# Half-row second passes in the scores of an encoder block: two query tiles side by side, odd tiles with the low part first

## The chip, the cores and the metric

The kernel runs on one core of a Trainium2 chip. The metric is the device time of one execution in microseconds (us), as the median of several runs. TensorE multiplies matrices, VectorE and ScalarE do elementwise work and read the accumulators in PSUM, GpSimd does elementwise work in SBUF, and SyncE issues most transfers.

## The reference

One encoder block over 1024 tokens of 1024 features, in float32: a layer norm, one wide projection, two attention branches, gates, an output projection, a second layer norm, a squared-ReLU MLP and a third layer norm. What matters here are the scores of the two branches:

```python
proj = h @ w_in[l] + b_in[l]
qa, ka, va, qb, kb, vb, ga, gb = jnp.split(proj, IN_SPLITS, axis=-1)
...
s = jnp.einsum('bwhd,bkwjhd->bhwkj', qr, kn).astype(jnp.float32) * scale
s = s + bias.astype(jnp.float32)[None]
...
s = jnp.einsum('bnqgrd,bnkgd->bngrqk', qb, kb).astype(jnp.float32) * (Dh ** -0.5)
s = jnp.where(valid[None, :, None, None], s, MASK_VALUE)
```

The first is neighbourhood attention (NA, 8 heads) on a 16 x 64 grid with a learned bias, the second windowed attention (SWA, 8 query heads, 2 key heads, rotary positions, a sink logit). Heads have 64 features.

## The kernel before, in words

Matmuls run in float32r, which keeps fewer bits than float32. Each operand is therefore split in a high part (the value rounded to float32r) and a low part (what the rounding left off), and a product is made of several matmuls that add up in PSUM. Weights and activations of the projections take three (`gemm3_steps`, L261: high x high, high x low, low x high, for 8 slices of the features).

Since a head has 64 features and TensorE takes 128 rows, the scores stack the parts. The tile `q` (128 x 1024) holds the high part of the queries in rows 0 to 63 and the low part in rows 64 to 127, or the other way round for the odd heads of SWA. The tiles `kh` and `kl` hold the keys' high and low part, each written twice, in both halves of the rows. A first pass `q` x `kh` (L506) then sums high x high and low x high, and a second pass `q` x `kl` (L507) adds high x low and low x low.

*Order of the work.* The attention stage lies about between 95 and 465 us. There are 64 steps: 16 heads (first 8 of SWA, then 8 of NA) times 4 pairs `t` of query tiles of 128 tokens. A tile looks at three tiles of keys (384 columns), the first and the last tile at two (256); so a step with t of 0 or 3 has one tile of each width, and the others have two of 384. `steps` (L717) works as a software pipeline whose order on every engine is as written:

- `part_a2(s + 1)` (L532): VectorE normalises the probabilities of the next step (L540, L543).
- `part_a(s + 2)` (L495): TensorE makes the scores of both tiles, each in a bank `ps_s` of its own (there are two), and VectorE adds bias or mask and takes the maximum (L509), which frees the bank; then the negated, scaled maximum goes to `st` (L513, L515).
- `pump` (L665): TensorE does some matmuls of the projections that later heads need, 12 a step in the SWA heads and 18 in the NA heads. They fill its time between the attention's matmuls.
- `part_b(s)` (L545): TensorE transposes the probabilities (L564), ScalarE copies them out (L567), VectorE makes the low part (L570). In between, `part_e(s + 2)` has ScalarE do the exponentials (L527, and L530 for the sinks).
- `part_c(s - 1)` (L573): probabilities x values (L599); at every second pair ScalarE (L605) and VectorE (L606) evacuate the output.

*How the queries come about.* A projection of 512 tokens (a half of the sequence) fills one bank `ps_mm`; there are two such banks, so the bank is asked for again one projection later. For NA (`proj_na_qk`, L312), 64 rows of the bank are queries and 64 are keys. ScalarE writes the queries' high part (L324) and the keys' high part twice (L325, L326); a few pumps later VectorE writes the queries' low part (L329) and the keys' low part (L331, which is the bank's last reader, and L333, a copy). For SWA (`proj_swa_q`, L403), one projection gives two heads; ScalarE evacuates the bank at once (L369), VectorE and GpSimd apply the rotary positions in SBUF, and some pumps later ScalarE copies the high parts (L414, two instructions, one a head) and VectorE subtracts for the low parts (L419, two instructions). All these are deferred by counts of pumps (`defer`, L274; D_NA, D_ROPE) and sit in the engines' queues between the steps' own instructions. Weights of the next projection are split on ScalarE (L457) and VectorE (L462).

Of the kernel before, what the change touches and what calls it, by code (L numbers as in the profile page):

```python
# [12 lines left out]
AF = mybir.ActivationFunctionType  # L13
ALU = mybir.AluOpType

P = 128
# [23 lines left out]
C_R = 98  # L40
N_PAR = 146

# [33 lines left out]
def encoder_block(ctx, tc, x, w_in, w_na, w_swa, w_out, w_ff1, w_ff2, par, rows, rpbp, sink,  # L76
# [4 lines left out]
    def b32(ap):  # L81
        return ap.bitcast(F32)
# [225 lines left out]
    def cols_na(h):  # L308
        return [(0, 8, 0, 64, w_in[:, h * 64:(h + 1) * 64]),
                (0, 8, 64, 64, w_in[:, 512 + h * 64:512 + (h + 1) * 64])]  # L310

    def proj_na_qk(h, w, store):  # L312
        q = ap.tile([P, S], F32R, tag="q", name="q", bufs=3)
        kh = ap.tile([P, S], F32R, tag="kh", name="kh")
        kl = ap.tile([P, S], F32R, tag="kl", name="kl")
        store.append((q, kh, kl))
        bq, bk = prm[0:64, C_QK + h:C_QK + h + 1], prm[64:P, C_QK + h:C_QK + h + 1]
        for half in range(2):
            cs = slice(half * 512, (half + 1) * 512)
            ps = psum("mm")  # L320
            yield from gemm3_steps(ps, w, lambda part, k: h_perm(part, k, half))

            def evac(cs=cs, ps=ps):
                ACT.activation(q[0:64, cs], ps[0:64, :], AF.Identity, bias=bq, scale=1.0)  # L324
                ACT.activation(kh[64:P, cs], ps[64:P, :], AF.Identity, bias=bk, scale=1.0)  # L325
                ACT.activation(kh[0:64, cs], ps[64:P, :], AF.Identity, bias=bk, scale=1.0)  # L326

            def evac2(cs=cs, ps=ps):
                DVE.scalar_tensor_tensor(out=q[64:P, cs], in0=ps[0:64, :], scalar=bq, in1=b32(q[0:64, cs]),  # L329
                                         op0=ALU.add, op1=ALU.subtract)  # L330
                DVE.scalar_tensor_tensor(out=kl[64:P, cs], in0=ps[64:P, :], scalar=bk, in1=b32(kh[64:P, cs]),  # L331
                                         op0=ALU.add, op1=ALU.subtract)
                DVE.tensor_copy(kl[0:64, cs], b32(kl[64:P, cs]))  # L333
            defer(0, evac, D_NA, evac2)
# [68 lines left out]
    def proj_swa_q(hp, w, store):  # L403
        qs = [ap.tile([P, S], F32R, tag="q", name="q", bufs=3) for _ in range(2)]
        store.extend(qs)
        for half in range(2):
            cs = slice(half * 512, (half + 1) * 512)
            ps = psum("mm")
            yield from gemm3_steps(ps, w, lambda part, k: h_nat(part, k, half))

            def hi(qf, cs=cs):
                for i in range(2):
                    a = slice(i * 64, i * 64 + 64)
                    ACT.copy(qs[i][a, cs], qf[a])  # L414

            def lo(qf, cs=cs):
                for i in range(2):
                    a, b = slice(i * 64, i * 64 + 64), slice(64 - i * 64, 128 - i * 64)
                    DVE.tensor_tensor(out=qs[i][b, cs], in0=qf[a], in1=b32(qs[i][a, cs]), op=ALU.subtract)  # L419
            rope(ps, prm[:, C_QB + hp:C_QB + hp + 1], half, (hi, lo))  # L420
# [74 lines left out]
    def part_a(s):  # L495
# [3 lines left out]
        st = ap.tile([P, 8], F32, tag="st", name="st", bufs=4)  # L499
        pns = []  # L500
        for i in range(2):
            j = 2 * t + i
            c0, c1 = max(j - 1, 0), min(j + 2, 8)
            n = (c1 - c0) * P
            ps = psum("s")
            PE.matmul(ps[:, :n], q[:, j * P:(j + 1) * P], kh[:, c0 * P:c1 * P], start=True, stop=False)  # L506
            PE.matmul(ps[:, :n], q[:, j * P:(j + 1) * P], kl[:, c0 * P:c1 * P], start=False, stop=True)  # L507
            p = ap.tile([P, 384], F32, tag="ss", name="ss", bufs=6)
# [1458 lines left out]
```

## Time and profile before

| What | us |
|---|---|
| Median of 3 runs | 1359.37 (1358.86 to 1360.43) |
| The profiled execution | 1356.82 |
| Its span in the trace | 1355.0 |
| TensorE busy | 1328.8 |
| VectorE busy | 991.9 |
| ScalarE busy | 705.1 |
| GpSimd busy | 275.4 |

The granted clock of TensorE is 0.998 over the span. The span is what lies between the first and the last instruction in the trace. PE is TensorE, DVE VectorE, ACT ScalarE, POOL GpSimd. A row of a group gives line, engine, operation, output<-inputs, shapes and count, then busy us and the mean ns of one, then the idle time before it and what ended that. Matmuls are pipelined and their ends are modelled, so that a busy TensorE isn't TensorE at its peak; the distance from one start to the next says more.

### The profile page before, as it was taken

Reading aid. Unit: us, or ns where it says so; the run is one execution under the profiler, and the core shown is the slowest. Engines: PE = TensorE matmul, PEld = TensorE weight load, DVE = VectorE, ACT = ScalarE, POOL = GpSimd, SP = SyncE. Lnnn points to the kernel's source line nnn. Section 1 sums busy time; section 2 is a strip of 40 time slices with the busy share of each in tenths; the row PEclk is TensorE's granted clock in tenths of the full one; section 3 lists DMA queues with packets and bytes.
Section 4 is the critical chain, followed back from the end, with each engine's and each line's share of the span. In section 5 each row is a group of like instructions: output and inputs, shape, how many; then the busy total and the mean of one; then the engine's idle time right before and its main releaser. Section 6 shows DMA issues by size and latency. Waiting matters only on the chain.

```text
span 1355.0 us, 17359 instructions
## 1 busy us (share of the span) xinstructions
PE 1328.8 (98%) x6299; PEld 1096.0 (81%) x6299; DVE 991.9 (73%) x1624; ACT 705.1 (52%) x1223; POOL 275.4 (20%) x260
## 2 busy tenths in 40 slices
PE   8999999999999999999999999999999999999997
PEld 6788888888888878888888788888887788888885
DVE  7658989877877896443678977677655668787777
ACT  5446667665665535531446755555554533333346
POOL 3322212121120000333630012222100001111207
PEclk9999999999999999999999999999999999999999
DMA  6531021112111433665244565665529554544323
GB/s 222 170 121 34 24 63 44 25 35 52 40 28 39 125 98 118 212 192 203 87 140 132 182 226 198 210 201 184 198 93 328 191 187 148 209 148 169 127 101 125
DMA packets 135798, 183.94 MB, mean 136 GB/s; under 512 B 27168, under 2 KB 85920, under 8 KB 132000
## 3 DMA queue, kind: packets, MB, share of 16 engines
q1 hardware_dynamic: 134992, 182.17, 40.6%
q8 instruction: 49, 0.80, 0.2%
q10 hardware_dynamic: 720, 0.67, 0.1%
q14 instruction: 37, 0.30, 0.1%
HBM read 126.69 MB, written 56.31 MB: 135 GB/s over the span
## 4 chain that ended last, share of the span: by engine, by line
PE 74%; DVE 16%; ACT 5%; issue 2%; DMA 2%; POOL 1%; SPq 0%; DVEq 0%; ACTq 0%; POOLq 0%
PE ps_mm L267 13%; PE ps_mm L1715 6%; PE ps_o L1283 6%; PE ps_mm L1283 6%; PE ps_t L1283 5%; PE ps_s L1715 5%; PE ps_t L1715 4%; PE ps_o L1715 4%; PE ps_s L1283 2%; DVE ss L543 2%; DVE ss L509 2%; ACT ss L527 2%; PE ps_o L599 2%; PE ps_mm L820 1%; PE ps_t L564 1%
## 5 line engine op out<-in xcount | busy, mean ns | idle before, releaser
L267 PE MATMUL ps_mm<-hT,whi 128*128 128x512 f32 x832 | 274.3, 404 | 6.2 <-POOL hT L243 3.3
L267 PEld LDWEIGHTS ps_mm<-hT,whi 128*128 128x128 f32 x832 | 154.0, 190 | 37.0 <-POOL hT L243 4.7
L267 PE MATMUL ps_mm<-hT,wlo 128*128 128x512 f32 x416 | 169.9, 408 | 1.0 <-DVE wlo L658 1.0
L527 ACT ACTIVATE ss<-ss,st 128x384 f32<-128x384 f32 (+1 forms) x128 | 74.5, 585 | 65.5 <-DVE st L515 34.7
L1583 ACT CAST t<-stg 128x2048 fp32r<-128x2048 f32 x28 | 53.4, 1908 | 87.6 <-PE ps_o L1715 47.0
L1715 PE MATMUL ps_mm<-t,t 128*128 128x512 f32 x384 | 91.7, 394 | 2.3 <-DVE t L1586 2.0
L1734 POOL TENSOR_TENSOR acc<-acc,rst 128x512 f32<-128x512 f32 x16 | 31.3, 1953 | 299.2 <-DMA rst<-xr_d 286.3
L1715 PE MATMUL ps_s<-t,t 128*128 128x512 f32 x384 | 90.8, 392 | 0.0
L267 PEld LDWEIGHTS ps_mm<-hT,wlo 128*128 128x128 f32 x416 | 78.8, 189 | 12.7 <-DVE wlo L658 1.4
L1715 PEld LDWEIGHTS ps_mm<-t,t 128*128 128x128 f32 x384 | 71.9, 188 | 19.6 <-DVE t L1586 2.9
L567 ACT CAST pth<-ps_t 128x384 fp32r<-128x384 f32 (+1 forms) x128 | 51.9, 456 | 66.1 <-PE ps_t L564 65.6
L1715 PEld LDWEIGHTS ps_s<-t,t 128*128 128x128 f32 x384 | 72.1, 188 | 16.1
L1283 PE MATMUL ps_t<-hS,tw 128*128 128x512 f32 x348 | 84.3, 391 | 0.0
L1283 PEld LDWEIGHTS ps_t<-hS,tw 128*128 128x128 f32 x348 | 65.3, 188 | 14.3
L1586 DVE TENSOR_TENSOR t<-stg,t 128x2048 fp32r<-128x2048 f32 x28 | 65.4, 2334 | 14.8 <-ACT t L1583 14.8
L1105 POOL TENSOR_TENSOR mx<-sg 128x512 f32<-128x512 f32 x16 | 33.5, 2094 | 190.6 <-DVE sg L1104 190.6
L1715 PE MATMUL ps_t<-t,t 128*128 128x512 f32 x288 | 68.8, 393 | 0.1
L1715 PE MATMUL ps_o<-t,t 128*128 128x512 f32 x288 | 67.8, 391 | 0.0
L570 DVE TENSOR_TENSOR ptl<-ps_t,pth 128x384 fp32r<-128x384 f32 (+1 forms) x128 | 61.1, 517 | 7.4 <-ACT pth L567 7.1
L1715 PEld LDWEIGHTS ps_t<-t,t 128*128 128x128 f32 x288 | 53.8, 188 | 13.1 <-DVE t L1586 1.3
L1715 PEld LDWEIGHTS ps_o<-t,t 128*128 128x128 f32 x288 | 54.1, 188 | 11.8
L1474 DVE TENSOR_TENSOR usl<-usl 128x512 f32<-128x512 f32 x64 | 50.8, 794 | 14.9 <-ACT usl L1367 11.7
(300 smaller groups left out, 3138.4 us busy)
## 6 DMA issues: line engine op xcount, KB each, us to landing
us_d<-usl SPq DMA_DIRECT2D x112, 256.0 KB
stg<-us_d SPq DMA_DIRECT2D x28, 1024.0 KB
raw<-in_w_ff SPq DMA_DIRECT2D x36, 512.0 KB
raw<-in_w_in SPq DMA_DIRECT2D x20, 512.0 KB
sg<-sg_d SPq DMA_DIRECT2D x32, 256.0 KB
w2b<-in_w_ff SPq DMA_DIRECT2D x7, 1024.0 KB
w2a<-in_w_ff SPq DMA_DIRECT2D x5, 1024.0 KB
sg_d<-sa SPq DMA_DIRECT2D x16, 256.0 KB
```

The costliest lines, as they stand in the source:

```text
L267: PE.matmul(ps, a[:, k, :], act(b, k), start=(k == 0 and i == 0), stop=(k == NK - 1 and i == 2))
L509: DVE.tensor_tensor_reduce(out=p[:, :n], in0=ps[:, :n], in1=bias_of(j), scale=1.0, scalar=NEG, op0=ALU.add, op1=ALU.max, accum_out=st[:, i ...
L527: ACT.activation(p[:, :n], p[:, :n], AF.Exp, bias=st[:, 2 + i:3 + i], scale=0.125, accum_out=st[:, 4 + i:5 + i])
L567: ACT.copy(pth[:, a:b, :], pv)
L570: DVE.tensor_tensor(out=ptl[:, a:b, :], in0=pv, in1=b32(pth[:, a:b, :]), op=ALU.subtract)
L1105: POOL.tensor_tensor(out=mx[:, f, half * 512:(half + 1) * 512], in0=both[0], in1=both[1], op=ALU.add)
L1283: PE.matmul(ps, ww, act[:, part, k, :], start=(first and k == 0 and m == 0), stop=(k == 3 and m == 2), skip_group_check=True)
L1474: DVE.tensor_tensor(out=out, in0=a, in1=b, op=op)
L1583: ACT.copy(slot[:, :, 0, :], src)
L1586: DVE.tensor_tensor(out=slot[:, :, 1, :], in0=src, in1=b32(slot[:, :, 0, :]), op=ALU.subtract)
L1715: PE.matmul(ps, st[:, a, part, j * P:(j + 1) * P], w[:, a, wpart, :], start=(first and a == 0 and m == 0), stop=(a == 3 and m == 2), skip_ ...
L1734: POOL.tensor_tensor(out=z, in0=z, in1=t, op=ALU.add)
```

## The change

Four things are changed.

1. `part_a` first makes the first pass of both tiles and then the second pass of both. The second pass takes only 64 of the 128 rows: rows 0 to 63 for the even tile of the step and rows 64 to 127 for the odd one. It adds high x low; low x low, which the full pass added, is no longer computed. The two second passes use different halves of the array's rows and different banks.
2. For that, the high part of the queries has to lie in rows 0 to 63 in even tiles and in rows 64 to 127 in odd tiles, for every head. `parity` picks the even or the odd tiles of a half of the sequence, as two blocks of 128 tokens.
3. In `proj_na_qk`, ScalarE's one write of the high part (64 x 512) becomes two of 64 x 256, and VectorE's one write of the low part becomes two. The bias of the queries is needed in rows 64 to 127 too, so the parameter table gets 8 columns (C_QO).
4. In `proj_swa_q`, ScalarE still copies the whole high part per head and then copies one parity of it into the other rows (64 x 256, one more instruction a head). VectorE's one subtraction per head becomes two of 64 x 256; one of them writes over the high part that it has read.

```diff
+    def parity(t, half, odd):
+        return t[:, half * 512:(half + 1) * 512].rearrange("p (j o f) -> p j o f", o=2, f=P)[:, :, odd]
...
         bq, bk = prm[0:64, C_QK + h:C_QK + h + 1], prm[64:P, C_QK + h:C_QK + h + 1]
+        bo = prm[64:P, C_QO + h:C_QO + h + 1]
...
-            def evac(cs=cs, ps=ps):
-                ACT.activation(q[0:64, cs], ps[0:64, :], AF.Identity, bias=bq, scale=1.0)
+            def evac(cs=cs, ps=ps, half=half):
+                for odd, rows_ in enumerate((slice(0, 64), slice(64, P))):
+                    ACT.activation(parity(q[rows_], half, odd), parity(ps[0:64], 0, odd), AF.Identity, bias=bq, scale=1.0)
...
-            def evac2(cs=cs, ps=ps):
-                DVE.scalar_tensor_tensor(out=q[64:P, cs], in0=ps[0:64, :], scalar=bq, in1=b32(q[0:64, cs]),
-                                         op0=ALU.add, op1=ALU.subtract)
+            def evac2(cs=cs, ps=ps, half=half):
+                for odd, (hi, lo, b) in enumerate(((slice(0, 64), slice(64, P), bq), (slice(64, P), slice(0, 64), bo))):
+                    DVE.scalar_tensor_tensor(out=parity(q[lo], half, odd), in0=parity(ps[0:64], 0, odd), scalar=b,
+                                             in1=parity(b32(q[hi]), half, odd), op0=ALU.add, op1=ALU.subtract)
...
-            def hi(qf, cs=cs):
-                for i in range(2):
-                    a = slice(i * 64, i * 64 + 64)
-                    ACT.copy(qs[i][a, cs], qf[a])
-
-            def lo(qf, cs=cs):
+            def hi(qf, cs=cs, half=half):
                 for i in range(2):
                     a, b = slice(i * 64, i * 64 + 64), slice(64 - i * 64, 128 - i * 64)
-                    DVE.tensor_tensor(out=qs[i][b, cs], in0=qf[a], in1=b32(qs[i][a, cs]), op=ALU.subtract)
+                    ACT.copy(qs[i][a, cs], qf[a])
+                    ACT.copy(parity(qs[i][b], half, 1 - i), parity(qf[a], 0, 1 - i))
+
+            def lo(qf, half=half):
+                for i in range(2):
+                    a, b = slice(i * 64, i * 64 + 64), slice(64 - i * 64, 128 - i * 64)
+                    for odd, to in ((i, b), (1 - i, a)):
+                        DVE.tensor_tensor(out=parity(qs[i][to], half, odd), in0=parity(qf[a], 0, odd),
+                                          in1=parity(b32(qs[i][a]), half, odd), op=ALU.subtract)
...
-        pns = []
+        pns, pss_ = [], []
...
-            ps = psum("s")
-            PE.matmul(ps[:, :n], q[:, j * P:(j + 1) * P], kh[:, c0 * P:c1 * P], start=True, stop=False)
-            PE.matmul(ps[:, :n], q[:, j * P:(j + 1) * P], kl[:, c0 * P:c1 * P], start=False, stop=True)
+            pss_.append((psum("s"), j, c0, c1, n))
+            PE.matmul(pss_[i][0][:, :n], q[:, j * P:(j + 1) * P], kh[:, c0 * P:c1 * P], start=True, stop=False)
+        for i, (ps, j, c0, c1, n) in enumerate(pss_):
+            rows_ = slice(i * 64, i * 64 + 64)
+            PE.matmul(ps[:, :n], q[rows_, j * P:(j + 1) * P], kl[rows_, c0 * P:c1 * P], start=False, stop=True)
+        for i, (ps, j, c0, c1, n) in enumerate(pss_):
```

The places that the change moves in the engines' queues are these. TensorE in a step with t = 3 of an SWA head, before (`ps_s` are the score banks, `ps_mm` a projection's, `kh` and `kl` the keys' parts, the last number the columns; the shape is the output's):

```order
L267 MATMUL ps_mm<-hT,wlo 128x512
L267 MATMUL ps_mm<-hT,whi 128x512 x2
L506 MATMUL ps_s<-kh,q 128x384
L507 MATMUL ps_s<-kl,q 128x384
L506 MATMUL ps_s<-kh,q 128x256
L507 MATMUL ps_s<-kl,q 128x256
L267 MATMUL ps_mm<-hT,wlo 128x512
L267 MATMUL ps_mm<-hT,whi 128x512 x2
```

and now:

```order
L268 MATMUL ps_mm<-hT,wlo 128x512
L268 MATMUL ps_mm<-hT,whi 128x512 x2
L519 MATMUL ps_s<-kh,q 128x384
L519 MATMUL ps_s<-kh,q 128x256
L522 MATMUL ps_s<-kl,q 128x384
L522 MATMUL ps_s<-kl,q 128x256
L268 MATMUL ps_mm<-hT,wlo 128x512
L268 MATMUL ps_mm<-hT,whi 128x512 x2
```

The second tile's first pass has moved ahead of the first tile's second pass, and the two second passes stand next to each other.

ScalarE between the exponentials of an SWA step and the next, where the second half of a pair of heads' queries is copied, before:

```order
L527 ACTIVATE ss,st<-ss,st 128x256
L530 ACTIVATE st<-st,snk 128x2
L414 CAST q<-qf 64x512 x2
L567 CAST pth<-ps_t 128x384 x2
L527 ACTIVATE ss,st<-ss,st 128x256
L527 ACTIVATE ss,st<-ss,st 128x384
L530 ACTIVATE st<-st,snk 128x2
L605 COPY oT<-ps_o 64x512
```

and now:

```order
L543 ACTIVATE ss,st<-ss,st 128x256
L546 ACTIVATE st<-st,snk 128x2
L424 CAST q<-qf 64x512
L425 CAST q<-qf 64x2x128
L424 CAST q<-qf 64x512
L425 CAST q<-qf 64x2x128
L583 CAST pth<-ps_t 128x384 x2
L543 ACTIVATE ss,st<-ss,st 128x256
L543 ACTIVATE ss,st<-ss,st 128x384
L546 ACTIVATE st<-st,snk 128x2
```

Two copies of 64 x 2 x 128 have come in ahead of the casts (`pth`) that a VectorE subtraction waits for.

VectorE at an evacuation of an NA projection, before (`oT` is the attention's output, `q` and `kl` the queries and the keys' low part):

```order
L570 TENSOR_TENSOR ptl<-ps_t,pth 128x384 x2
L606 TENSOR_TENSOR oT<-ps_o,oT 64x512
L329 SCALAR_TENSOR_TENSOR q<-ps_mm,prm,q 64x512
L331 SCALAR_TENSOR_TENSOR kl<-ps_mm,prm,kh 64x512
L333 CAST kl<-kl 64x512
```

and now:

```order
L586 TENSOR_TENSOR ptl<-ps_t,pth 128x384 x2
L622 TENSOR_TENSOR oT<-ps_o,oT 64x512
L339 SCALAR_TENSOR_TENSOR q<-ps_mm,prm,q 64x2x128 x2
L341 SCALAR_TENSOR_TENSOR kl<-ps_mm,prm,kh 64x512
L343 CAST kl<-kl 64x512
```

The bank's last reader, once L331 and now L341, stands behind two half-wide instructions instead of one whole one.

More of the change, by code (lines that the diff above doesn't have):

```diff
@@ L40 @@
 C_R = 98
-N_PAR = 146
+C_QO = 146
+N_PAR = 154
 N_AHEAD = 4
@@ L1946 @@
                                       a["b_ff2"][0])),
+        np.roll(qk, 64, axis=0),
     ], axis=1)
```

## The prediction

> **What bounds the kernel now.** I read the page first for the whole, then the waits and the chain of waits of the attention stage (95 to 465 us, where all 128 edited matmuls lie), then durations by shape and the timeline at the edited places.
>
> ```profile
> span 1355.0 us, 17359 instructions
> PE 1328.8 (98%) x6299; PEld 1096.0 (81%) x6299; DVE 991.9 (73%) x1624; ACT 705.1 (52%) x1223; POOL 275.4 (20%) x260
> ```
>
> By busy time TensorE is the bound, but its ends are modelled, so that says little. The waits of the stage are more telling (waiter, what it waited for, total us, times, longest):
>
> ```profile
> PE ps_s L506 <- DVE st L509: 2.4, 3, 1.2
> PE ps_mm L267 <- DVE kl L331: 2.1, 5, 1.1
> ```
>
> TensorE hardly waits, and where it does, it is for VectorE to give back a bank of PSUM: the score bank in the first half of the stage, the projection bank in the second. The chain of waits (start, us, engine, tile, line) shows which engine sets the pace in between. First the windowed (SWA) heads:
>
> ```profile
> 108.20 0.34 PE ps_t L564 x3
> ```
>
> ```profile
> 171.76 0.34 DVE ss L509
> ...
> 172.40 1.20 ACT ss L527 x4
> ...
> 263.82 0.77 DVE kl L331
> 264.63 0.73 PE ps_mm L267 x2
> ```
>
> Up to 108.2 us TensorE leads. From there to 264.6 us I take the path as a loop between VectorE and ScalarE: reduction (L509), exponential (L527), scaling (L543), and VectorE's other work in its fixed order; TensorE runs ahead and is stopped once per pair of heads. Only from 131 to 157 us does the chain name TensorE, and I read that as a tie, since the ScalarE copy that is said to wait for it there starts just as ScalarE's instruction before it ends:
>
> ```profile
> 156.68 0.28 ACT L530 ACTIVATE st<-st,snk 128x2 f32<-128x2 f32 x1
> 156.98 0.58 ACT L605 COPY oT<-ps_o 64x512 f32<-64x512 f32 x1
> ```
>
> In the neighbourhood (NA) heads the pattern is another:
>
> ```profile
> 300.57 0.34 PE ps_t L564 x3
> ...
> 300.99 0.86 ACT pth L567 x2
> ...
> 302.94 0.57 ACT q L324
> ...
> 304.94 0.74 DVE q L329
> ...
> 310.19 0.57 ACT q L324
> ...
> 313.50 0.74 DVE q L329
> ...
> 314.26 0.77 DVE kl L331
> ...
> 315.07 0.73 PE ps_mm L267 x2
> ```
>
> TensorE leads from 264.6 to 300.9, then 14 us of ScalarE and VectorE, two evacuations of projections among them (L324, L329), lead until the bank comes back at 315.07. The cycle comes three times, once per pair of heads (with the last two evacuations of the SWA part these are the five waits of the row above); after it TensorE leads.
>
> **The change part by part.** *TensorE.* What a second pass costs is the distance from its start to the next start:
>
> ```profile
> 305.07 0.28 PE L507 MATMUL ps_s<-kl,q 128*128 128x256 f32 x1
> 305.19 0.34 PE L506 MATMUL ps_s<-kh,q 128*128 128x384 f32 x1
> 305.37 0.34 PE L507 MATMUL ps_s<-kl,q 128*128 128x384 f32 x1
> 305.54 0.39 PE L267 MATMUL ps_mm<-hT,wlo 128*128 128x512 f32 x1
> ```
>
> 0.12 us at 256 columns, 0.17 at 384. If the two half-row matmuls of a step run beside each other, the shorter is hidden: 32 steps (t of 1 or 2) save 0.17 and 32 save 0.12, 9.3 us in all, 0.145 a step. No row of before has a 64-row matmul; the bounds are 0.145 saved and, with the array emptied at both switches, a loss: the last row but one is busy 0.34 for 0.17 of distance, so emptying is about 0.17, twice 0.34, less 0.145 is 0.195 lost a step. I take the saving, since the narrow matmuls that the kernel already mixes in show no such gap:
>
> ```profile
> 302.90 0.28 PE L599 MATMUL ps_o<-pth,vv 128*128 128x256 f32 x1
> 303.02 0.28 PE L599 MATMUL ps_o<-ptl,vv 128*64 128x256 f32 x1
> ```
>
> 0.12 apart, like two full ones of 256 columns. (That is 64 columns, not 64 rows, so the row is near, not the same.) The Trainium skill, "TensorE: Matmul & The Clock Gate", Part 3, says that matmuls on different row groups run concurrently, starting about 4 ns apart; no run here shows it, and by it the saving is the one I take.
>
> The new order also lets VectorE's first reduction of a step start up to 0.17 us later (three matmuls ahead of it instead of two) and asks for the second score bank 0.17 earlier. In SWA VectorE comes to its reductions after they are ready, and in NA the loop's next lead is TensorE's own, so both cost nothing; without that cover they would cost 0.17 a step where VectorE waits for scores.
>
> *VectorE and ScalarE.* Every write of the queries' two parts is cut in two of half the width, and the windowed queries get an extra copy. Prices:
>
> ```profile
> L570 DVE TENSOR_TENSOR ptl<-ps_t,pth 128x384 fp32r<-128x384 f32 x96 | 50.2, 550 | 5.9 <-ACT pth L567 5.7
> L570 DVE TENSOR_TENSOR ptl<-ps_t,pth 128x256 fp32r<-128x256 f32 x32 | 13.3, 417 | 1.5 <-ACT pth L567 1.4
> L567 ACT CAST pth<-ps_t 128x384 fp32r<-128x384 f32 x96 | 43.0, 483 | 58.8 <-PE ps_t L564 58.5
> L567 ACT CAST pth<-ps_t 128x256 fp32r<-128x256 f32 x32 | 12.0, 375 | 7.3 <-PE ps_t L564 7.1
> L329 DVE SCALAR_TENSOR_TENSOR q<-ps_mm,prm,q 64x512 fp32r<-64x512 f32 x16 | 11.9, 745 | 3.5 <-ACT kh L326 3.2
> L324 ACT ACTIVATE q<-ps_mm,prm 64x512 fp32r<-64x512 f32 x16 | 10.8, 674 | 0.1
> L414 ACT CAST q<-qf 64x512 fp32r<-64x512 f32 x12 | 7.3, 611 | 0.1
> L419 DVE TENSOR_TENSOR q<-qf,q x16: 684/687/1676, 87.2 to 218.4; 64x512 fp32r<-64x512 f32 x16
> ```
>
> VectorE's slope is (550-417)/128 = 1.04 ns an element, ScalarE's (483-375)/128 = 0.84; 256 elements fewer are 266 and 216 ns. So a half of L419 is 687-266 = 421 and the pair costs +0.155 us; a half of L329 is 479, the pair +0.21; a half of L324 is 458, the pair +0.24; the extra copy is 611-216 = 395, two of them +0.79 a half of SEQ. Bounds for a half-wide instruction: half the old price (nothing added) and a whole one.
>
> *SWA, 108 to 264.6.* VectorE sets the pace, so TensorE's saving there is worth nothing, and the 4 steps before 108 give -0.58. VectorE's additions count in full: six halves of queries fall here, 12 x 0.155 = 1.86; the first four NA evacuations, 4 x 0.21 = 0.85; ScalarE's 0.24 once, where L605 and behind it VectorE's L606 queue behind L324 just before 264.6. The extra copies stand ahead of the casts that VectorE subtracts from:
>
> ```profile
> 133.12 1.23 ACT L414 CAST q<-qf 64x512 fp32r<-64x512 f32 x2
> 134.38 0.86 ACT L567 CAST pth<-ps_t 128x384 fp32r<-128x384 f32 x2
> ...
> ```
>
> ```profile
> 135.31 1.01 DVE L570 TENSOR_TENSOR ptl<-ps_t,pth 128x384 fp32r<-128x384 f32 x2
> ```
>
> Moved by 0.79, the first cast ends at 134.38+0.79+0.48 = 135.65 where VectorE wants it at 135.31: +0.34, three times (one half in each pair of heads; at the other half VectorE comes to the casts later, and I add nothing): 1.0. Sum: 1.86+0.85+0.24+1.0-0.58 = +3.4.
>
> *NA, three cycles.* In the 14 us that ScalarE and VectorE lead, two evacuations add 2 x (0.24+0.21) = +0.90. In the part that TensorE leads, a bank that came back just in time now comes late:
>
> ```profile
> 286.50 0.68 DVE L606 TENSOR_TENSOR oT<-ps_o,oT 64x512 f32<-64x512 f32 x1 [1.75 <-ACT oT L605]
> 295.73 0.42 DVE L570 TENSOR_TENSOR ptl<-ps_t,pth 128x256 fp32r<-128x256 f32 x1 [0.26 <-ACT pth L567]
> ...
> 297.45 0.76 DVE L331 SCALAR_TENSOR_TENSOR kl<-ps_mm,prm,kh 64x512 fp32r<-64x512 f32 x1
> ```
>
> ```profile
> 298.43 0.62 PE L267 MATMUL ps_mm<-hT,whi 128*128 128x512 f32 x2
> ```
>
> L331 ends at 298.21, the bank is used again at 298.43: 0.22 of room. Two evacuations stand in that chain too: VectorE waits for ScalarE behind each (the rows at 286.50 and 295.73), so L331 ends 2 x (0.24+0.21) = 0.90 later, 0.68 past the old use, whatever TensorE saved since the first of the two. The three steps before that save 0.44, and one after the bank's return 0.15. A cycle: -0.44+0.68-0.15+0.90 = +0.99, three +3.0. If that bank stays in time, the cycle is about nothing (six steps, -0.87, against +0.90). The last six steps, TensorE's own, save 0.87.
>
> Sum: 3.4+3.0-0.9 = +5.5 us. The profiled execution took 1356.8 us (span 1355.0 and 1.8 around it), 2.6 under the median of the three runs, 1359.4. Forecast: 1359.4+5.5 = 1364.9. The parameter table's 8 more columns are one transfer long before; I cost them at nothing.
>
> **The rivals.** *Faster.* The halves cost half (no fixed part shows at 64 partitions), ScalarE's copies hide, and only TensorE's saving is left where it leads: -0.58, 3 x -0.87, -0.87 is -4.1, 1355.3. For it: TensorE is 98% busy and named by most of the chain. Against: each pair of widths above shows a fixed part. With the additions (9.6 us between this sum and the forecast's) scaled by f, the total is -4.1+9.6f: it turns at f = 0.43.
>
> *It cancels.* f between 0.15 and 0.7, so that the total is within 2.7 us of 1359.4; or all prices hold and the bank used at 298.43 stays in time in every cycle (3.4+0.1-0.9 = +2.6, 1362.0).
>
> *Serial.* The half-row matmuls queue one behind the other, as the old ones did: nothing saved, SWA +3.95, each cycle 0.68+0.90, three 4.7: +8.7, 1368.1.
>
> *Emptying.* Each switch between full and half rows costs 0.17 as worked out above: 4 steps before 108 +0.8, SWA +3.95, a cycle 3 x 0.195 + (0.90-0.22-2 x 0.195) + 0.195 + 0.90 = 2.0, three 5.9, the last six steps +1.2: +11.8, 1371.2. For it: nothing in before switches rows. Against: the 0.12 above. The Trainium skill, "TensorEngine Tiling (Array Packing)", Key Properties, says that changing the tiling mode drains the engine; before's 64-column rows do not show a gap, and no run here tries rows.
>
> **How the numbers follow.** Forecast 0.45, serial 0.15, emptying 0.15, cancelling 0.15, faster 0.10. What this kernel's measurement can tell from no change is about 0.2%, 2.7 us. Faster: 0.10. Within: the cancelling case and the forecast's lower edge, 0.20. Slower: 0.70. The range goes from 1358.5 (leaving out the faster case and some of the cancelling one) to 1370.5 (half of the emptying case outside).
>
> **What would show it.** Right: in the chain of the changed kernel SWA stays VectorE and ScalarE, with 264.6 moved to about 268; half-wide rows of 0.42 to 0.48 us; second passes starting within 0.02 us of each other and 0.17 to the next; TensorE's waits for the projection bank up from 2.1 to about 5 us. Wrong: half-wide rows near 0.35; SWA shorter than before (then TensorE led there); a gap of 0.1 or more at each switch (then emptying); the 298.43 kind of wait not there.

## The result and the profile after

The changed kernel takes 1379.63 us (median of 4 runs, 1378.67 to 1380.47), the kernel before 1359.9 beside it: 1.0145 times as long, 95% interval 1.0132 to 1.0157, or +19.7 us. The forecast was +5.5 (1364.9, range to 1370.5). The direction was right; the size was not, and lies beyond the worst rival (1371.2). The profiled execution took 1379.96 us. The page of the profile:

```profile
span 1378.2 us, 17425 instructions
PE 1349.5 (98%) x6299; PEld 1085.0 (79%) x6299; DVE 999.9 (73%) x1656; ACT 716.0 (52%) x1255; POOL 273.0 (20%) x260
```

TensorE is now said to be busy for 20.7 us more, though half the rows of 128 matmuls went away. The waits of the attention stage (95 to 485 us now) show two rows that were as good as absent before:

```profile
PEld ps_s L522 <- issue: 14.0, 64, 0.3
PEld ps_mm L268 <- issue: 13.8, 67, 0.7
...
PEld ps_mm L268 <- DVE kl L341: 4.8, 4, 1.5
...
PE ps_mm L268 <- DVE kl L341: 3.8, 7, 1.1
```

PEld is the load of weights. 64 times, once a step, it stands idle for 0.22 us in front of the half-row pass, and as often again in front of the first projection matmul behind it, and nothing that the profile shows releases it. The timeline of one step shows what that is. First the kernel before (a step of two 384-column tiles; matmuls, then the weight loads):

```profile
317.81 0.33 PE L506 MATMUL ps_s<-kh,q 128*128 128x384 f32 x1
317.99 0.34 PE L507 MATMUL ps_s<-kl,q 128*128 128x384 f32 x1
318.16 0.34 PE L506 MATMUL ps_s<-kh,q 128*128 128x384 f32 x1
318.34 0.35 PE L507 MATMUL ps_s<-kl,q 128*128 128x384 f32 x1
318.52 0.40 PE L267 MATMUL ps_mm<-hT,wlo 128*128 128x512 f32 x1
...
319.45 0.60 PE L564 MATMUL ps_t<-ident,ss 128*128 128x128 f32 x4
```

```profile
318.16 0.19 PEld L507 LDWEIGHTS ps_s<-kl,q 128*128 128x128 f32 x1
318.34 0.19 PEld L267 LDWEIGHTS ps_mm<-hT,wlo 128*128 128x128 f32 x1
```

and the same step now:

```profile
327.10 0.51 PE L519 MATMUL ps_s<-kh,q 128*128 128x384 f32 x2
327.54 0.45 PE L522 MATMUL ps_s<-kl,q 64*128 64x384 f32 x2
327.92 0.50 PE L268 MATMUL ps_mm<-hT,wlo 128*128 128x512 f32 x1
...
328.94 0.60 PE L580 MATMUL ps_t<-ident,ss 128*128 128x128 f32 x4
```

```profile
327.54 0.19 PEld L522 LDWEIGHTS ps_s<-kl,q 64*128 64x128 f32 x2 [0.25 <-issue]
327.91 0.19 PEld L268 LDWEIGHTS ps_mm<-hT,wlo 128*128 128x128 f32 x1 [0.19 <-issue]
```

Three things are to be seen. The two half-row passes do run beside each other: both weight loads lie within 0.19 us, and the next matmul starts 0.38 behind the pair. Before, a load started 0.18 ahead of its matmul, under the matmul in front of it; at a change between full and half rows, and back, load and matmul start together (327.54 twice, 327.91 and 327.92). And there is a wait ahead of the load. So from the first pass to the transposes the step takes 1.84 us, where it took 1.64: +0.20. In a step with a 256-column tile less is hidden, and it is +0.28 (from the first pass to the second projection matmul behind the scores 1.10 us, before 0.82).

The Trainium skill says both things ("TensorE: Matmul & The Clock Gate", Part 3: matmuls on different rows of the array start about 4 ns apart; "TensorEngine Tiling (Array Packing)", Key Properties: a change of the tiling mode drains the engine). The trace agrees with the first, and with the second where the rows change; a change to 64 columns and back shows no gap (0.12, as the prediction's rows have it). The page gives no price; it is about 0.19 us a switch, which the runs below count.

The cycles of the NA heads show up as the bank's returns to TensorE in the chain of waits, which before stood at 264.63, 315.07 and:

```profile
365.50 0.74 PE ps_mm L267 x2
```

```profile
415.96 0.73 PE ps_mm L267 x2
```

50.4 us apart. Now:

```profile
270.92 0.73 PE ps_mm L268 x2
```

```profile
324.36 0.73 PE ps_mm L268 x2
```

```profile
377.79 0.73 PE ps_mm L268 x2
```

```profile
431.24 0.73 PE ps_mm L268 x2
```

They are 53.4 apart: +3.0 a cycle, 9.0 in three, where the forecast had 1.0 a cycle. Up to 270.92 it is +6.3, of which 1.4 stood there before any score was made (the first pass of the scores starts at 96.8, before at 95.4). The prices of the narrow instructions are close to those forecast (478, 464 and 438 ns, for 479, 458 and 421):

```profile
L339 DVE SCALAR_TENSOR_TENSOR q<-ps_mm,prm,q 64x256 fp32r<-64x256 f32 x32 | 15.3, 478 | 4.7 <-ACT kh L335 4.2
L333 ACT ACTIVATE q<-ps_mm,prm 64x256 fp32r<-64x256 f32 x32 | 14.9, 464 | 0.3
L431 DVE TENSOR_TENSOR q<-qf,q 64x256 fp32r<-64x256 f32 x28 | 12.3, 438 | 0.5
```

Some time went where nothing was edited. The mixing stage's matmuls (L257 before, L258 now), with min/median/max ns of one and the start of the first and the last; before, then now:

```profile
L257 PE MATMUL ps_o<-oS,whi x64: 393/394/395, 541.5 to 626.0; 128*128 128x512 f32 x64
```

```profile
L258 PE MATMUL ps_o<-oS,whi x64: 393/395/397, 558.7 to 644.8; 128*128 128x512 f32 x64
```

84.5 us have become 86.1. The MLP's first product (L1283, now L1299) does the same: 722.4 to 1032.4 before, 741.1 to 1052.8 now, 310.0 and 311.7. Together +3.3 us.

The two profiled executions differ by 23.1 us, the medians by 19.7, since the profiled one of before is 3.1 under its median. The differences at the start (1.4) and behind 1033 us (2.8) are also there, with 1.3 and 1.8, in the run e9_low_half, which edits neither place; I count them as what one execution differs from another.

### The profile page after: what moved, and what is told of

Read it like the earlier page. It is cut to its first block, busy times and chain, and to the rows that moved or that the text cites. A ratio compares the mean times of both kernels' runs of the same rounds, so it can differ in the third digit from the quotient of the medians.

```text
span 1378.2 us, 17425 instructions
## 1 busy us (share of the span) xinstructions
PE 1349.5 (98%) x6299; PEld 1085.0 (79%) x6299; DVE 999.9 (73%) x1656; ACT 716.0 (52%) x1255; POOL 273.0 (20%) x260
## 4 chain that ended last, share of the span: by engine, by line
PE 71%; DVE 16%; ACT 8%; DMA 2%; issue 2%; POOL 1%; SPq 0%; DVEq 0%; ACTq 0%; POOLq 0%
PE ps_mm L268 11%; PE ps_mm L1731 6%; PE ps_o L1299 6%; PE ps_mm L1299 5%; PE ps_s L1731 5%; PE ps_t L1299 5%; PE ps_t L1731 4%; PE ps_o L1731 4%; PE ps_s L1299 2%; ACT ss L543 2%; DVE ss L559 2%; DVE ss L525 2%; PE ps_mm L836 1%; PE ps_o L615 1%; PE ps_s L1188 1%
## 5 line engine op out<-in xcount | busy, mean ns | idle before, releaser
L268 PE MATMUL ps_mm<-hT,wlo 128*128 128x512 f32 x416 | 176.5, 424 | 1.0 <-DVE wlo L674 1.0
L1599 ACT CAST t<-stg 128x2048 fp32r<-128x2048 f32 x28 | 53.4, 1909 | 88.0 <-PE ps_o L1731 47.3
L1299 PE MATMUL ps_t<-hS,tw 128*128 128x512 f32 x348 | 84.8, 392 | 0.0
L1299 PEld LDWEIGHTS ps_t<-hS,tw 128*128 128x128 f32 x348 | 65.3, 188 | 14.8
L1490 DVE TENSOR_TENSOR usl<-usl 128x512 f32<-128x512 f32 x64 | 50.4, 788 | 16.1 <-ACT usl L1383 11.7
```

The costliest lines, as they stand in the source:

```text
L268: PE.matmul(ps, a[:, k, :], act(b, k), start=(k == 0 and i == 0), stop=(k == NK - 1 and i == 2))
L1299: PE.matmul(ps, ww, act[:, part, k, :], start=(first and k == 0 and m == 0), stop=(k == 3 and m == 2), skip_group_check=True)
L1490: DVE.tensor_tensor(out=out, in0=a, in1=b, op=op)
L1599: ACT.copy(slot[:, :, 0, :], src)
```

## The experiments

The theory after the result has three parts that add up: each switch between full and half rows costs about 0.20 us on TensorE; the split writes of the queries cost what the serial rival summed; and the table's 8 columns slow TensorE in stages that the change doesn't touch, because they move tiles in SBUF. The rivals are those of the prediction, and for the last part that the drift is chance.

| Run | Median, us | Ratio to before, 95% interval |
|---|---|---|
| e1_columns | 1363.46 | 1.0023 (1.0014 to 1.0032) |
| e2_layout | 1372.80 | 1.0098 (1.0084 to 1.0112) |
| e3_rows | 1368.86 | 1.0058 (1.0044 to 1.0071) |
| e4_one_half | 1376.34 | 1.0117 (1.0103 to 1.0131) |
| e5_four_switches | 1401.44 | 1.0296 (1.0281 to 1.0310) |
| e6_sixteen_columns | 1365.50 | 1.0040 (1.0026 to 1.0055) |
| e7_windowed_splits | 1362.95 | 1.0018 (1.0009 to 1.0027) |
| e8_neighbourhood_splits | 1363.60 | 1.0027 (1.0016 to 1.0038) |
| e9_low_half | 1357.06 | 0.9975 (0.9967 to 0.9984) |
| e10_before_sixteen | 1351.16 | 0.9931 (0.9919 to 0.9944) |
| e11_before_thirtytwo | 1362.04 | 1.0013 (1.0004 to 1.0022) |
| e12_low_half_sixteen | 1348.39 | 0.9910 (0.9895 to 0.9925) |

The kernel before had medians of 1360.17 to 1360.20 us beside them.

**The columns alone** (e1_columns; before with the longer table).

```diff
-N_PAR = 146
+N_PAR = 154
...
+        np.roll(qk, 64, axis=0),
```

> The kernel before with nothing but the 8 more columns in the parameter table (not read by anything), which move most tiles in SBUF by 32 bytes. Theory A (switching): the loss is made in the attention stage by the switches between full and half rows; then this is within 1 us of before, and the 6 to 7 us that the changed trace is longer outside that stage (1.4 at the start, the rest in the mixing stage and the MLP, where nothing is edited) are differences between executions. Theory C (placement): the moved tiles make matmuls outside the attention stage about 2% longer; then this is 4 to 6 us slower than before, and the matmuls of the mixing stage start 233 ns apart instead of 229.

+3.3 us, between theory A's 1 and theory C's 4 to 6. The stages have the changed kernel's times to a tenth (L257's row from 542.9 to 629.0, 86.1; the MLP's product from 725.4 to 1037.0, 311.6), and the attention is as before (0.2 us of drift). The forecast's "cost at nothing" was wrong.

**The queries' layout alone** (e2_layout; with the columns, all passes on 128 rows, in the old order; the edit is against the changed kernel).

```diff
-        for i, (ps, j, c0, c1, n) in enumerate(pss_):
-            rows_ = slice(i * 64, i * 64 + 64)
-            PE.matmul(ps[:, :n], q[rows_, j * P:(j + 1) * P], kl[rows_, c0 * P:c1 * P], start=False, stop=True)
+            PE.matmul(ps[:, :n], q[:, j * P:(j + 1) * P], kl[:, c0 * P:c1 * P], start=False, stop=True)
```

> The changed kernel with the scores' matmuls of before: both passes on all 128 rows, one tile after the other; the queries lie as in the change, with its split writes and extra copies. Theory B (the forecast's mechanism: VectorE and ScalarE pay for the split writes): +3.9 us in the windowed heads and +1.6 in each of the three cycles of the neighbourhood heads, +8.7 in all (plus 4 to 6 if the placement counts). Theory A: the windowed heads +3.9, since VectorE sets the pace there, but most of the 10 us that the changed kernel loses in the neighbourhood heads is the switches', so +4 to +7 in all (plus the placement's part).

+12.6 us, 9.3 of it beside the columns' 3.3; the serial rival summed 8.7. The banks' returns:

```profile
321.72 0.73 PE ps_mm L268 x2
```

```profile
426.54 0.73 PE ps_mm L268 x2
```

Two cycles in 104.82, 52.4 each: +2.0 a cycle, where that rival had 0.68 + 0.90 = 1.58. The windowed part is +3.9, for 3.95.

**The rows alone** (e3_rows; before's layout, so that half of the tiles multiply low x low instead of high x low, of the same size).

```diff
-            PE.matmul(ps[:, :n], q[:, j * P:(j + 1) * P], kl[:, c0 * P:c1 * P], start=False, stop=True)
...
+        for i, (ps, j, c0, c1, n) in enumerate(pss_):
+            rows_ = slice(i * 64, i * 64 + 64)
+            PE.matmul(ps[:, :n], q[rows_, j * P:(j + 1) * P], kl[rows_, c0 * P:c1 * P], start=False, stop=True)
```

> The kernel before with the change's matmul order and half-row second passes, but the queries written as before: in half of the tiles the second pass then multiplies the low part of the queries with the keys' low part instead of the high part with it. Theory A: a step costs TensorE 0.25 us more (the array empties at both switches and the weight loads beside them are not hidden); the 34 steps in which TensorE leads pay 8 us, the windowed heads about 0 to 1, so +8 to +9. Theory B: TensorE saves 0.145 us a step where it leads and VectorE has nothing added, so -4 us.

+8.7 us: TensorE's saving is a loss even when VectorE and ScalarE have nothing more to do. Mixing and MLP are as before. A cycle is +1.5. In this run's chain of waits all eight steps of a cycle are TensorE's, and eight times 0.24 (the mean of 0.20 and 0.28) is 1.9. Against that stands what before lost once a cycle, where the bank came late:

```profile
364.90 0.40 PE L267 MATMUL ps_mm<-hT,wlo 128*128 128x512 f32 x1
365.50 0.74 PE L267 MATMUL ps_mm<-hT,whi 128*128 128x512 f32 x2 [0.20 <-DVE kl L331]
```

From 364.90 to the third start behind it, at 366.07, are 1.17 us, where three starts 0.23 apart take 0.70: 0.47, which this run doesn't lose. The waits of the stage:

```profile
PEld ps_s L509 <- issue: 14.0, 64, 0.3
PEld ps_mm L267 <- issue: 11.8, 64, 0.2
```

**Both passes on the same half** (e4_one_half; two switches, nothing side by side; the edit is against the run before it).

```diff
-            rows_ = slice(i * 64, i * 64 + 64)
+            rows_ = slice(s // 4 % 2 * 64, s // 4 % 2 * 64 + 64) if s < 32 else slice(0, 64)
```

> As the run before, but both second passes of a step use the same half of the rows, the one in which the high part lies as before (rows 0 to 63 in the neighbourhood heads and the even windowed heads, 64 to 127 in the odd ones), so that they cannot run beside each other; all that is needed is computed. Theory A: the switches are paid as in the run before and nothing is hidden, so a step costs 0.15 to 0.17 us more than there: +13 to +14 us. If the switches cost nothing, it is like before, within 1 us.

+16.2 us, above the 13 to 14 expected. The step of two 384-column tiles, and the loads:

```profile
328.74 0.51 PE L506 MATMUL ps_s<-kh,q 128*128 128x384 f32 x2
329.18 0.61 PE L509 MATMUL ps_s<-kl,q 64*128 64x384 f32 x2
329.72 0.50 PE L267 MATMUL ps_mm<-hT,wlo 128*128 128x512 f32 x1
...
330.75 0.71 PE L567 MATMUL ps_t<-ident,ss 128*128 128x128 f32 x5
```

```profile
329.18 0.29 PEld L509 LDWEIGHTS ps_s<-kl,q 64*128 64x128 f32 x2 [0.25 <-issue]
```

The pair takes 0.54 us instead of 0.38, and the step 2.01: 0.37 over before, 0.17 over the changed kernel. So running side by side does save the 0.17 that the forecast counted on, and the switches take back twice that. The second half-row pass starts 0.28 after the first, not 0.17. The first one's own load, which is in the open, makes the difference: the second's starts 0.17 ahead of its matmul, under the first pass, as between two full passes:

```profile
329.28 0.19 PEld L509 LDWEIGHTS ps_s<-kl,q 64*128 64x128 f32 x1
```

```profile
329.45 0.34 PE L509 MATMUL ps_s<-kl,q 64*128 64x384 f32 x1
```

So between two half-row passes no switch is paid. A cycle is +2.55: eight steps of 0.38 (0.37, and 0.39 with a 256-column tile), less the 0.47 of the bank.

**Four switches** (e5_four_switches; the edit is against before).

```diff
-            PE.matmul(ps[:, :n], q[:, j * P:(j + 1) * P], kl[:, c0 * P:c1 * P], start=False, stop=True)
+            rows_ = slice(s // 4 % 2 * 64, s // 4 % 2 * 64 + 64) if s < 32 else slice(0, 64)
+            PE.matmul(ps[:, :n], q[rows_, j * P:(j + 1) * P], kl[rows_, c0 * P:c1 * P], start=False, stop=True)
```

> The kernel before with only one edit: the second pass of each tile takes 64 rows (those with the queries' high part, in before's layout of the rows) and stays where it was, right behind its own first pass. A step then goes full, half, full, half, full: four switches instead of the changed kernel's two, no two half-row passes side by side. Low x low is left out. Theory (each switch between full and half rows costs about 0.2 us: about 0.10 of waiting and 0.107 of a weight load that is no longer hidden): per step 4 x 0.2 = 0.8 us more than before, where TensorE leads. The run with both passes on one half (two switches) had +7.9 us from its attention for 34 steps on which TensorE leads (18 in the neighbourhood heads, 16 others partly hidden); here I expect the neighbourhood cycles at 4 to 5 us each instead of 3, and +28 us in all (1388), between +22 and +38, since part of the windowed heads becomes TensorE-led. Rival (the cost is one per step, whatever the number of switches, for instance only the way back to full rows in front of a projection): like the run with both passes on one half, +16 us (1376). Second rival (a half-row pass is itself slow, and the switch is free): like the one-half run or below, +13 to +16.

+41.2 us, above the +22 to +38 that I gave, and far from both rivals. A cycle is +5.7 (4 to 5 expected; eight steps of 0.77, less 0.47), and the windowed heads lose 20 us, 0.6 a step, which says that TensorE leads through most of them now; I had allowed for less. 64 x 0.8 = 51 is what it would be if none hid. The idle time in front of half-row loads has doubled (112 of 128 such waits recorded), and the second tile's first pass now waits too:

```profile
PEld ps_s L508 <- issue: 27.7, 112, 0.4
PEld ps_mm L267 <- issue: 8.8, 48, 0.2
PEld ps_s L507 <- issue: 7.0, 38, 0.2
```

A step with one 256-column tile, from its first pass to the second projection matmul behind the scores:

```profile
329.59 0.28 PE L507 MATMUL ps_s<-kh,q 128*128 128x256 f32 x1
...
331.18 0.63 PE L267 MATMUL ps_mm<-hT,whi 128*128 128x512 f32 x2
```

1.59 us, before 0.82: 0.77 for four switches, where the run with both passes on one half has 0.38 for two. That is 0.19 each. The two runs have the same number of half-row matmuls, so the cost goes with the number of switches.

**The windowed splits alone** (e7_windowed_splits; before's table; all passes on 128 rows).

```diff
+                    ACT.copy(parity(qs[i][b], half, 1 - i), parity(qf[a], 0, 1 - i))
...
-                    DVE.tensor_tensor(out=qs[i][b, cs], in0=qf[a], in1=b32(qs[i][a, cs]), op=ALU.subtract)
+                    for odd, to in ((i, b), (1 - i, a)):
+                        DVE.tensor_tensor(out=parity(qs[i][to], half, odd), in0=parity(qf[a], 0, odd),
+                                          in1=parity(b32(qs[i][a]), half, odd), op=ALU.subtract)
```

> The kernel before with one part of the change: the windowed heads' queries in the new layout (the extra copy of one parity on ScalarE, VectorE's subtraction in two halves), the neighbourhood heads' queries as before, all second passes on 128 rows, the parameter table as before. The computation is the reference's. Theory (additions on VectorE's path through the windowed heads, as the prediction sums them): 12 x 0.155 + 1.0 = +2.9 us, 1363.0 (1.0021), all of it between 108 and 265 us, nothing in the neighbourhood cycles. Rival (the extra copies' delay of the casts is hidden or the halves cost half): 0 to +1. Rival (the additions reach further than the path's own sum, by waits of TensorE for the banks): +5 or more.

+2.75 us, for 2.9, all of it before 265 us. The terms 1.86 and 1.0 stand as a sum.

**The neighbourhood splits alone** (e8_neighbourhood_splits; both halves into the same rows as before).

```diff
+                for odd in range(2):
+                    ACT.activation(parity(q[0:64], half, odd), parity(ps[0:64], 0, odd), AF.Identity, bias=bq, scale=1.0)
...
+                for odd in range(2):
+                    DVE.scalar_tensor_tensor(out=parity(q[64:P], half, odd), in0=parity(ps[0:64], 0, odd), scalar=bq,
+                                             in1=parity(b32(q[0:64]), half, odd), op0=ALU.add, op1=ALU.subtract)
```

> The kernel before with one part of the change: in the neighbourhood heads each write of the queries' high part (ScalarE) and low part (VectorE) is cut in two of half the width, one for the even and one for the odd tiles, into the same rows as before. All else, the second passes on 128 rows too, is as before; the computation is the reference's. Theory (additions as the prediction sums them, with nothing saved on TensorE): 0.85 + 0.24 in the windowed part and 3 x 1.58 in the cycles, +5.8 us, 1366.0 (1.0043). With e2's measured 1.96 a cycle instead of 1.58 it is +7.0 (1.0051). Rival (the halves cost half, or the bank's return has more room than the rows showed): +1 to +2. This run and the one with the windowed splits together should make the 9.3 us that the whole new layout cost without its 8 columns.

+3.4 us, between the theory and its rival, and 3 us short of what the two runs were to make together. The timeline of VectorE at the third cycle's end says why. This run, then the changed kernel:

```profile
419.54 0.87 DVE L335 SCALAR_TENSOR_TENSOR q<-ps_mm,prm,q 64x256 fp32r<-64x256 f32 x2
420.42 0.76 DVE L337 SCALAR_TENSOR_TENSOR kl<-ps_mm,prm,kh 64x512 fp32r<-64x512 f32 x1
421.21 0.42 DVE L339 CAST kl<-kl 64x512 fp32r<-64x512 f32 x1
```

```profile
429.44 0.97 DVE L339 SCALAR_TENSOR_TENSOR q<-ps_mm,prm,q 64x256 fp32r<-64x256 f32 x2
430.43 0.76 DVE L341 SCALAR_TENSOR_TENSOR kl<-ps_mm,prm,kh 64x512 fp32r<-64x512 f32 x1
```

Two halves into the same rows take 0.87 us together, two into different rows 0.97, though one by itself takes about as long in both (474 and 478 ns). ScalarE's pair does the same (0.72 in this run's chain of waits, 0.36 and 0.47 in the changed kernel's). An evacuation gets 0.26 longer here and 0.50 there, and a cycle has four in its path: measured +1.1 here (51.5 us) and +2.0 in the run of the layout. So my run wasn't the pure part of the change that I took it for. The Trainium skill has a rule for VectorE ("VectorE: DVE Perf Modes", Two Vector instructions with no wait between them): an instruction whose output, or whose first input from SBUF, starts in another group of 32 rows than that of the instruction before is held until all before it have finished. These rows agree with it; in the changed kernel the second half's output and its input from SBUF both change rows, so they don't tell the two apart.

**Sixteen columns** (e6_sixteen_columns; the changed kernel, 8 columns more).

```diff
-N_PAR = 154
+N_PAR = 162
...
+        np.zeros((128, 8), np.float32),
```

> The changed kernel with 16 instead of 8 more columns in the parameter table (8 of them dead), so that the tiles behind it in SBUF move by 64 bytes and not by 32. Theory (tiles at unlike places within 64 bytes make the mixing stage and the first MLP product 2% slower): those two stages go back to before's times, -1.7 us each, and the kernel to 1376.3, 3.3 less than the changed kernel (ratio to before about 1.0120); the attention stage stays as in the changed kernel. Rival (any move of the tiles costs it, or the load of a longer table): 1379.6 to 1383 (1.0145 to 1.017).

+5.3 us over before and 14.1 under the changed kernel, where I expected 3.3. The attention is the same (its start and its end are both about 1 us earlier); everything behind it is faster than in before. L257's row (here L258):

```profile
L258 PE MATMUL ps_o<-oS,whi x64: 389/389/390, 557.2 to 640.8; 128*128 128x512 f32 x64
```

83.6 us, and every one of the 64 takes 389 or 390 ns. From one start to the next the stage's matmuls are 226.7 ns apart, in before 228.9 and in the changed kernel 233.3. The program's own allocation shows the tiles' places: before, most tiles of weights and activations lie 32 bytes past a multiple of 128, and those that are allocated from the right side 96. The mixing stage's product has one tile of each kind. With 8 columns it is 64 and 96, with 16 it is 96 and 96. This asked for three more runs.

**Before with 16 dead columns, and with 32** (e10_before_sixteen, e11_before_thirtytwo; for 32 the number is 178).

```diff
-N_PAR = 146
+N_PAR = 162
...
+        np.zeros((128, 16), np.float32),
```

> The kernel before with 16 dead columns in the parameter table and nothing else: the tiles on the left side of SBUF move by 64 bytes, which puts the weights' and the moving tiles of every product behind the attention at the same place within 128 bytes (96 and 96; before 32 and 96, with 8 columns 64 and 96). Theory (unlike places make a matmul of 512 columns 228 to 234 ns instead of 226.7): the stages behind 500 us lose what the changed kernel with 16 columns lost there against before, about 7.7 us, and the attention stays: 1352.5 (0.9943). Rival (that loss belongs to something else of the changed kernel, not to the place): 1360 to 1361 (1.000).

-9.0 us, for -7.7, the most of all single edits, and it computes nothing else:

```profile
L257 PE MATMUL ps_o<-oS,whi x64: 389/389/389, 542.7 to 626.3; 128*128 128x512 f32 x64
```

The mixing stage takes 83.6 us and the MLP's first product 307.1 (720.3 to 1027.4), for 84.5 and 310.0.

> The kernel before with 32 dead columns: the left side moves by 128 bytes. Theory (only the place within 128 bytes counts): 32 and 96 again, so like before, 1360.2 (ratio 0.999 to 1.001), every stage's spacing as in before. Rival (a longer move or a longer table helps by itself): like 16 columns, 1352.5 or below. Second rival (each move costs, as 8 columns did): 1363 or more.

+1.8 us, and neither as before nor as the rivals have it:

```profile
L257 PE MATMUL ps_o<-oS,whi x64: 394/394/394, 543.3 to 629.4; 128*128 128x512 f32 x64
```

86.1 us, the slow value of 8 columns, though the places are 32 and 96 as in before. That the place within 128 bytes is all that counts is thereby refuted. What the runs do show is one side of it: with weights and moving tile at the same place within 128 bytes every stage behind the attention was fast, in three kernels; with unlike places it was slower, by an amount that the place within 128 bytes doesn't settle. In the attention stage the place doesn't show: weights and moving tile of its projections lie at the same place in every kernel (32, 64 or 96), and their matmuls start 230 to 232 ns apart in all of them.

**Less for VectorE instead of TensorE**, alone (e9_low_half) and with 16 columns (e12_low_half_sixteen).

```diff
-        kl = ap.tile([P, S], F32R, tag="kl", name="kl")
+        if h < 2:
+            na_kl.append(ap.tile([P, S], F32R, tag="kl", name="kl"))
+            POOL.memset(b32(na_kl[h][64:P]), 0.0)
+        kl = na_kl[h % 2]
...
-                DVE.scalar_tensor_tensor(out=kl[64:P, cs], in0=ps[64:P, :], scalar=bk, in1=b32(kh[64:P, cs]),
+                DVE.scalar_tensor_tensor(out=kl[0:64, cs], in0=ps[64:P, :], scalar=bk, in1=b32(kh[64:P, cs]),
...
-                DVE.tensor_copy(kl[0:64, cs], b32(kl[64:P, cs]))
```

> The kernel before with one edit that takes work off VectorE instead of TensorE: for the neighbourhood heads the keys' low part is written into rows 0 to 63 alone, in one instruction, and the copy into the other rows (L333) goes; rows 64 to 127 of the two tiles are zero, set once by GpSimd. The second pass stays on 128 rows, so no switch, and low x low is left out in these heads, as in the changed kernel. Theory (VectorE's path from 108 to 265 us and the neighbourhood chains count in full): 0.42 us saved for each of the first four evacuations and 0.42 once in each of the three cycles, where L333 stands in the chain: -1.7 - 1.3 = -3 us, 1357.2 (0.9978). Rival (L333 has cover, since it stands behind the bank's last reader L331): 0 to -1, 1359.5 (0.9995).

-3.1 us, for -3: leaving out low x low does pay when it is taken off the engines that lead. A cycle is 0.5 shorter (0.42 expected), the windowed part 1.0 (1.7 expected), so that the total came out this close in part by luck.

> Both together, meant to be faster than both kernels: the kernel before with the neighbourhood keys' low part in rows 0 to 63 alone (low x low left out there) and 16 dead columns in the parameter table. Theory (the two act in different stages and add): -3.0 - 7.7 = -10.7 us, 1349.5 (0.9921). Rival (only the place counts): 1352.5 (0.9943).

-11.8 us, for -10.7: the two add, and this kernel beats both, by 0.9% and by 2.3%.

## Why the prediction was wrong in size

*The step that failed* is "I take the saving, since the narrow matmuls that the kernel already mixes in show no such gap". 64 columns are not 64 rows: the 128*64 matmuls show no gap, the 64-row ones wait and show their weight load at each switch. The step was to be 0.145 us shorter; it is 0.20 to 0.28 longer, 0.24 in the mean. The prediction's own sign for this, a gap of 0.1 or more at each switch, is what the trace shows. The Trainium skill's rule against the change stood in the emptying rival, at a chance of 0.15. That rival's 0.195 a step is near the price partly by luck: it counted an emptied array alone, and about half of a switch's 0.19 is the weight load in the open, which the prediction didn't have. I weighed a near row as if it were the same.

*The sum of the emptying rival* was still 8 us short. Its cycle had 2.0 us, by a term in which TensorE's loss gives the bank time to come back (-0.39); the runs show no such relief: 2.0 (layout) plus four steps of 0.24 is 3.0, as measured, and the changed kernel's chain of waits does name four of TensorE's steps in a cycle (327.26, 333.99, 340.33 and 360.51 us). The steps up to the first evacuation of a cycle and those behind the bank's return all count. My reading of why, that the evacuation starts when TensorE's projection is done and so the bank moves with TensorE, no run tests by itself.

*The windowed part*: forecast +3.4, measured +4.9. The additions of VectorE and ScalarE were right (3.9, for 3.95); the four steps ahead of 108 us have the wrong sign (+1.1, not -0.6).

*The cycles*: forecast 1.0 each, measured 3.0. Of the 2.0 missing, TensorE's steps are 1.6 (-0.44 - 0.15 turned into four losses of 0.24), and 0.4 are the splits, 2.0 for 1.58: 0.50 instead of 0.45 four times, and the 0.22 of room hid nothing. The last six steps: -0.9 forecast, +1.6 measured (from the bank's last return to the last matmul of L599, now L615, 49.2 us before and 50.8 now).

*The columns*: "I cost them at nothing", measured +3.3. The transfer shows no cost (the attention of the run with the columns alone is as before); the moved tiles do.

The parts nearly add up: 3.3 (columns) + 9.3 (layout) + 8.7 (rows) = 21.3, against 19.7.

*What was right*: that SWA is set mostly by VectorE and ScalarE (with the rows alone it still got 2.0 us longer from its fifth step on), that the two passes run side by side, the prices of halves and of the extra copy, and the bank that comes late: TensorE's wait for it grew from 2.1 to 3.8 us (about 5 forecast), and to 8.0 in the run of the layout, where no switch slows TensorE.

## What to carry to other kernels

A matmul on part of the rows was paid for where half rows began and where they ended, about 0.19 us each time here, so half-row passes should do better in long runs than in pairs between full ones; no run here has more than two in a row. Before an engine's saving is counted, see which engine leads there: low x low left out on VectorE's side (neighbourhood heads alone) gained 3 us, on TensorE's side it lost. When an edit makes a constant tile longer, look at the spacing of matmuls in stages that it doesn't touch.

## What the runs showed of the hardware

- A switch between 128-row and 64-row matmuls cost 0.19 us: a wait of about 0.09, and 0.107 of a weight load that is not hidden. From a 384-column full pass to a half-row one it is 0.27 us, where two full ones are 0.17 apart.
- Two half-row matmuls on the same half were 0.28 us apart, 0.107 of it the first one's load in the open; the second's load ran under the first matmul. On different halves they started together (0.003 apart).
- Where a product's weights and its moving tile lay in SBUF made a 512-column matmul's record in the mixing stage 389 ns or up to 397, and 9.0 us of this kernel. Equal places within 128 bytes were fast in every stage behind the attention; why unlike ones differ among themselves, and why the attention's projections show no difference, stays open.
- A pair of half-wide instructions that write the same rows was 0.10 us shorter on VectorE (0.87, for 0.97) and 0.11 on ScalarE (0.72, for 0.83 in the chains of waits) than a pair that writes different ones.
